# A two-layer trunk on one core: turned blocks fetched by SP's queue, work at fixed chunk distances, a buffer for the weights' turns

## The chip, the cores and the metric

The kernel runs on one core of one Trainium2 chip. The metric is the device time of one execution in microseconds. TensorE (PE) multiplies, VectorE (DVE) and ScalarE (ACT) do elementwise work, GpSimd (POOL) small arithmetic, and SyncE (SP) issues most transfers. Each engine takes its instructions in order.

## The reference

256 tokens of width 2048 pass two layers, each `h = h + Mixer(RMSNorm(h))`. Layer 1 is a gated DeltaNet. Layer 2, which the change touches, is banded softmax attention with 16 heads of 128; at 256 tokens the band holds every earlier chunk, so a frame sees its own 64-frame chunk and all before:

```
proj = h @ w_in                                  # q, k, v, gate z, 2048 wide each
q = rms_norm(q, q_norm_w); k = rms_norm(k, k_norm_w)
s = einsum('bchd,bmhd->bhcm', q_n, k_n) * scale + bias
p = softmax(where(valid, s, -inf))
o = einsum('bhcm,bmhd->bchd', p, v_n)
out = (o * silu(z)) @ w_out
```

All is float32.

## The kernel before

**Weights.** All weights (some 170 MB) are read once, in chunks of 512 KB. `fetch` (line 183) brings chunk after chunk on SP's queue into one of four buffers `wt`, ACT rounds it to a high part (`whi`, line 207, "the cast") and DVE subtracts for the low part (`wlo`, line 208). High and low parts have three buffers each. `chunk` (line 288) multiplies a chunk with the activations, which are split in the same way: three products. A wide chunk in layer 2 is twelve matmuls of 128x512. When chunk i is written, fetches up to i + 3 are written too, and `state["use"]` counts the chunks begun.

**The order.** Small work is written as generators in two lanes, `bgq` and `bg2`. A chunk gives two steps (`tick`); a step advances one lane, in turn, and a generator that yields 0 passes its step on. `behind` ties the work of a step behind the last matmul and the next chunk's cast and subtraction. The places on each engine follow from that when the program is built.

**Layer 2.** Its wide blocks have eight chunks each: keys and queries of a group of four heads in turn (K0, Q0, K1, Q1 to K3, Q3), then the values V0 to V3. That makes 96 chunks, numbered here from 0: K0 is 0 to 7, Q0 8 to 15, K1 16 to 23 and so on. The tokens lie on the partitions there; scores need the head's width on them. So a block is *turned*: DVE transposes it in pieces of 32x32 (line 1082), one DMA writes it to a scratch tensor in HBM (the *trip*, line 1053), and four DMAs *fetch* it back, 32 partitions each (line 1055). Both are issued by POOL, in `regroup`.

`qk_norm` (line 1058) is the chain of one K or Q block: square (ACT, line 1063), sum (DVE, 1066), reciprocal root (POOL, 1068 and 1070), normalising (DVE, 1075), turning, trip, fetch. Keys are fetched straight to `kn`; queries to a buffer `g` with the tag `cv`, from which ACT writes `qn` with a scale (line 1092, the *scaling pass*). `attend` (line 1095) is the chain of a group's four heads: scores (PE, 1112 and 1113; DVE 1122; ACT's exponentials, 1126), weights (DVE, 1132 and 1134), their turns by pairs of heads (DVE, 1141) with trip and fetch. It begins 11 chunks (`LEAD`) after its first step, and a step is one head. `values` (line 1166) multiplies weights by values.

The tag `cv` has two buffers, which squares, normalised blocks, turned blocks, `g` and the turned weights share. `kn`, `qn` and the values lie in the 48 KB slot `dl` (`hmem["m"]`), `kn` and `qn` with two places each.

Of the kernel before, what the change touches and what calls it, by code (L numbers as in the profile page):

```python
# [17 lines left out]
H = 16  # L18
# [6 lines left out]
LEAD = 11  # L25
# [14 lines left out]
def tile_hybrid_trunk(  # L40
# [11 lines left out]
    nc = tc.nc  # L52
# [35 lines left out]
    ps = ps_small()  # L88
# [74 lines left out]
    fetched, splits, state = {}, {}, {"next": 0, "use": 0, "mm": None}  # L163
# [52 lines left out]
    bgq, bg2, now = [], [], []  # L216
# [723 lines left out]
    for gi in range(4):  # L940
        ps = pair(xb, 2)
# [6 lines left out]
    hmem = {}  # L948
# [36 lines left out]
    bmem = {}  # L985

    def b_setup():
        scales["h"] = yield from row_scales(hmem["s"], "rh")
        ssh2 = scales["h"][2]
        uh = const.tile([P, 2], F32, name="uh")  # L990
        pool.tensor_scalar(out=uh, in0=ssh2, scalar1=1.0 / D, scalar2=EPS, op0=ALU.mult, op1=ALU.add)
        pool.tensor_scalar(out=uh, in0=uh, scalar1=EPS, scalar2=None, op0=ALU.mult)
        wqk = const.tile([P, 1], F32, name="wqk")
        pool.tensor_scalar(out=wqk, in0=sm[:, C_QW:C_QW + 1], scalar1=sm[:, C_KW:C_KW + 1],
                           scalar2=float(P) ** -0.5, op0=ALU.mult, op1=ALU.mult)
        bias = hmem["m"][:, 2 * D:4 * D].rearrange("p (h k) -> p h k", h=H)
# [49 lines left out]

    trips = [0]

    def regroup(dst, u):

        trips[0] += 1
        m = rows.tile([P, 4, 32 * u.shape[1]], F32, name="trip%d" % trips[0])
        nc.gpsimd.dma_start(out=m, in_=u.rearrange("p x c j -> p c (x j)"))
        for c in range(4):
            nc.gpsimd.dma_start(out=dst[32 * c:32 * c + 32].rearrange("i r x j -> i r (x j)"),  # L1055
                                in_=m[:, c, :].rearrange("(r i) y -> i r y", r=4))

    def qk_norm(ps, scale, dst):

        ssn = tiny.tile([P, 2, 4], F32, name="ssn", tag="so")  # L1060
        rn = tiny.tile([P, 2, 4], F32, name="rn", tag="ro")
        sq = wk("cv").rearrange("p h t -> p (h t)")
        act.activation(out=sq, in_=ps.rearrange("p t d -> p (t d)"), func=AF.Square)
        yield 1
        yield 1
        dve.reduce_sum(out=ssn, in_=sq.rearrange("p (t h d) -> p t h d", t=2, d=P), axis=AX.X)
# [3 lines left out]
        pool.tensor_tensor(out=rn, in0=ssn, in1=nhalf[:, :8].rearrange("p (t h) -> p t h", t=2), op=ALU.pow)  # L1070
        yield 1
        yield 1
        n = wk("cv").rearrange("p h t -> p (h t)").rearrange("p (t d) -> p t d", t=2)
        for t in range(2):
            dve.tensor_tensor(out=n[:, t, :].rearrange("p (h d) -> p h d", d=P),  # L1075
                              in0=ps[:, t, :].rearrange("p (h d) -> p h d", d=P),
                              in1=rn[:, t, :].unsqueeze(2).broadcast_to([P, 4, P]), op=ALU.mult)
        yield 1
        yield 1
        u = wk("cv").rearrange("p h t -> p (h t)").rearrange("p (c x j) -> p x c j", c=4, j=32)  # L1080
        for t in range(2):
            dve.transpose(out=u[:, 4 * t:4 * t + 4], in_=n[:, t, :].rearrange("p (x c i) -> p x c i", c=4, i=32))
            yield 1
        if scale is None:
            regroup(dst, u)
            yield 1
            return
        g = wk("cv").rearrange("p h t -> p (h t)").rearrange("p (r x j) -> p r x j", r=4, j=32)
        regroup(g, u)
        yield 1  # L1090
        yield 1
        act.activation(out=dst.rearrange("p x (r j) -> p r x j", r=4), in_=g, func=AF.Copy, scale=scale)
        yield 1

    def attend(gi, qn, kn):
        if gi == 0:
            gated_tiles()
            gmem["done"] = 0
            bmem["groups"] = 0
            bmem["w"] = slot("kT", 16)  # L1100
        st = {}
        first = state["use"] + LEAD
        while state["use"] < first:
            yield 0
# [30 lines left out]

        def turned(i):
            if i % 2 == 0:
                u = wk("cv").rearrange("p h t -> p (h t)")[:, :768]
                st["u"] = u.rearrange("p (c x j) -> p x c j", c=4, j=32)
            x = 3 * (i % 2)  # L1140
            dve.transpose(out=st["u"][:, x:x + 3], in_=st[i][0].rearrange("p (x c i) -> p x c i", c=4, i=32))
            if i % 2:
                regroup(weights_of((4 * gi + i) // 2), st["u"])

        stages = (scores, weights, turned)
        for n in range(4 + len(stages) - 1):
            for k in reversed(range(len(stages))):
                if 0 <= n - k < 4:
                    stages[k](n - k)
            yield 1  # L1150
        bmem["groups"] = gi + 1

    def weights_of(pr):

        w = bmem["w"][:, 768 * pr:768 * pr + 768] if pr < 5 else hmem["m"][:, 2 * D + 768 * (pr - 5):2 * D + 768 * (pr - 4)]
        return w.rearrange("p (r x j) -> p r x j", r=4, j=32)

    def vb_small(gi, ps):
        c = (8192, 10240, 9216, 11264)[gi]
        v = hmem["m"][:, c:c + 1024].rearrange("p (t d) -> p t d", t=2)  # L1160
        bmem["v"] = v
        for t in range(2):
            act.activation(out=v[:, t, :], in_=ps[:, t, :], func=AF.Copy, scale=scales["h"][0][:, t:t + 1])
        yield 1
# [33 lines left out]

    for gi in range(4):
# [30 lines left out]
    ps = [ps_small().rearrange("p (a t) -> p a t", a=2) for _ in range(2)]  # L1230
# [68 lines left out]
```

## Time and profile before

| | |
|---|---|
| median of 3 runs | 993.3 us (990.38 to 993.48) |
| the profiled execution | 992.0 us, its span 990.3 us |
| granted TensorE clock | 1.00 |
| DMA | 194.34 MB, mean 196 GB/s |
| ACT busy, POOL busy | 525.4 us, 114.8 us |
| chain that ended last | PE 85%, DMA 6%, DVE 3% |

Layer 2's wide blocks run from about 608 to 895 us. A row of the timeline has the start, the time taken, engine, line, operation, what it writes and reads, and in brackets the idle time of its engine before it and what ended that. Matmuls overlap, and their ends are modelled. A row of the stretches has the stretch, its length, the busy time and count of PE, PEld (weight loads), DVE, ACT and POOL, the granted clock, the busy share of the DMA engines and GB/s. DMAs issued by POOL appear as `trip<-cv` (the trip) and `cv<-trip`, `dl<-trip`, `kT<-trip` (fetches of queries, keys or weights, and weights).

### The profile page before, as it was taken

How to read it: one execution, taken by the hardware profiler on the slowest of the kernel's cores; microseconds unless marked ns; L12 is line 12 of the kernel's file. 1: busy time of each engine (PE TensorE's matmuls, PEld its weight loads, DVE VectorE, ACT ScalarE, POOL GpSimd, SP SyncE). 2: the span in 40 equal slices, each digit the busy share in tenths (PEclk: the TensorE clock that was granted, in tenths of full speed). 3: DMA queues.
4: the chain of work that ended last, by engine and by line, in shares of the span. 5: the costliest groups of instructions: out<-in, count | busy, mean ns of one | idle time of the engine just before them, and what ended most of it. 6: DMA issues, size and time to landing. Idle time of an engine off the chain costs nothing.

```text
span 990.3 us, 15268 instructions
## 1 busy us (share of the span) xinstructions
PE 979.2 (99%) x5803; PEld 849.7 (86%) x5803; DVE 699.5 (71%) x1146; ACT 525.4 (53%) x741; POOL 114.8 (12%) x177
## 2 busy tenths in 40 slices
PE   9999999999999999999999999999999999999998
PEld 7988888888888899899888888887788878888887
DVE  7789787997999768665767555555767766555544
ACT  8456887645547646444554444444454545444442
POOL 1002100122000001110000000122424240100000
PEclk9999999999999999999999999999999999999999
DMA  9668675545665553447765767686888786755672
GB/s 292 192 171 240 208 208 159 164 139 181 175 192 170 147 149 107 128 149 224 225 190 177 231 209 212 188 258 180 273 248 275 240 280 184 219 182 170 211 218 85
DMA packets 143817, 194.34 MB, mean 196 GB/s; under 512 B 9328, under 2 KB 100352, under 8 KB 143744
## 3 DMA queue, kind: packets, MB, share of 16 engines
q1 hardware_dynamic: 136832, 172.12, 57.4%
q0 software_dynamic: 6624, 20.99, 6.9%
q8 instruction: 45, 0.74, 0.3%
q10 hardware_dynamic: 288, 0.26, 0.1%
q14 instruction: 28, 0.23, 0.1%
HBM read 183.90 MB, written 9.45 MB: 195 GB/s over the span
## 4 chain that ended last, share of the span: by engine, by line
PE 85%; DMA 6%; DVE 3%; issue 2%; ACT 2%; POOL 2%; SPq 0%; ACTq 0%; DVEq 0%; POOLq 0%
PE psp L256 76%; DMA trip<-cv 3%; PE pss L602 2%; DVE wlo L208 1%; ACT whi L207 1%; DMA wt<-in_a_w_in_dram 1%; DMA wt<-in_b_w_in_dram 1%; PE pss L256 1%; PE pss L839 1%; PE pss L1175 1%; POOL rn L1070 1%; DMA cv<-trip 1%; DMA g<-in_xT_dram 1%; POOL ssn L1068 0%; PE pss L1113 0%
## 5 line engine op out<-in xcount | busy, mean ns | idle before, releaser
L208 DVE TENSOR_TENSOR wlo<-wt,whi 128x1024 fp32r<-128x1024 f32 (+2 forms) x324 | 390.0, 1208 | 222.7 <-ACT whi L207 221.3
L207 ACT CAST whi<-wt 128x1024 fp32r<-128x1024 f32 (+2 forms) x324 | 335.8, 1039 | 354.3 <-PE psp L256 309.0
L256 PE MATMUL psp<-whi,xb 128*128 128x512 f32 x1024 | 323.9, 394 | 0.4 <-ACT whi L207 0.4
L256 PE MATMUL psp<-xb,whi 128*128 128x512 f32 (+1 forms) x1088 | 257.5, 380 | 0.6 <-ACT whi L207 0.4
L256 PEld LDWEIGHTS psp<-whi,xb 128*128 128x128 f32 x1024 | 192.0, 188 | 39.9 <-ACT whi L207 0.8
L256 PEld LDWEIGHTS psp<-xb,whi 128*128 128x128 f32 x1088 | 195.3, 189 | 34.8 <-DVE ev L327 0.6
L256 PE MATMUL psp<-wlo,xb 128*128 128x512 f32 x512 | 200.8, 392 | 4.2 <-DVE wlo L208 4.2
L256 PE MATMUL psp<-xb,wlo 128*128 128x256 f32 x1024 | 147.3, 284 | 0.8 <-DVE wlo L208 0.5
L256 PEld LDWEIGHTS psp<-xb,wlo 128*128 128x128 f32 x1024 | 136.6, 191 | 7.2 <-DVE wlo L208 2.0
L256 PE MATMUL psp<-g,whi 128*128 128x512 f32 (+1 forms) x608 | 131.6, 346 | 0.2 <-DVE ev L327 0.2
L256 PEld LDWEIGHTS psp<-wlo,xb 128*128 128x128 f32 x512 | 96.2, 188 | 26.2 <-DVE wlo L208 6.8
L256 PEld LDWEIGHTS psp<-g,whi 128*128 128x128 f32 x608 | 104.4, 190 | 13.0 <-DVE ev L327 0.6
L256 PE MATMUL psp<-g,wlo 128*128 128x256 f32 x480 | 82.2, 283 | 0.0
L256 PEld LDWEIGHTS psp<-g,wlo 128*128 128x128 f32 x480 | 69.8, 191 | 1.8
L519 DVE SCALAR_TENSOR_TENSOR cv<-raw,sm,cv 128x255 f32<-128x255 f32 (+2 forms) x144 | 63.9, 480 | 5.2 <-ACT cv L517 4.9
L517 ACT ACTIVATE cv<-raw,sm 128x256 f32<-128x256 f32 x48 | 22.2, 501 | 10.4 <-DVE raw L342 10.4
L327 DVE TENSOR_TENSOR ev<-psp,ev 128x512 f32<-128x512 f32 x37 | 25.3, 683 | 0.1
L326 ACT COPY ev<-psp 128x512 f32<-128x512 f32 x37 | 21.4, 579 | 2.5 <-DVE raw L342 2.5
L874 POOL TENSOR_TENSOR ro<-so,nhalf 128x8 f32<-128x8 f32 x4 | 8.4, 2107 | 122.4 <-DVE so L872 122.4
L1075 DVE TENSOR_TENSOR cv<-psp,rn 128x512 f32<-128x512 f32 x16 | 10.3, 685 | 12.4 <-POOL rn L1070 12.4
L1055 POOL DMA_DIRECT2D dl<-trip x28 | 15.4, 558 | 27.8 <-DMA trip<-cv 22.4
L1126 ACT ACTIVATE raw<-raw,mx 128x128 f32<-128x128 f32 (+1 forms) x32 | 14.3, 446 | 7.6 <-DVE mx L1124 7.6
(245 smaller groups left out, 750.5 us busy)
## 6 DMA issues: line engine op xcount, KB each, us to landing
wt<-in_b_w_in_dram SPq DMA_DIRECT2D x128, 512.0 KB, 4.4
wt<-in_a_w_in_dram SPq DMA_DIRECT2D x125, 512.0 KB, 4.0
wt<-in_a_w_out_dram SPq DMA_DIRECT2D x32, 512.0 KB, 3.7
wt<-in_b_w_out_dram SPq DMA_DIRECT2D x32, 512.0 KB, 3.4
trip<-cv POOLq DMA_DIRECT2D x8, 512.0 KB, 5.3
trip<-cv POOLq DMA_DIRECT2D x8, 384.0 KB, 4.3
tt<-line POOLq DMA_DIRECT2D x4, 512.0 KB, 9.5
dl<-in_xT_dram POOLq DMA_DIRECT2D x4, 512.0 KB, 6.5
```

The costliest lines, as they stand in the source:

```text
L207: cast = act.copy(out=hi[:, js, cs], in_=wt[:, js, cs])
L208: rest = dve.tensor_tensor(out=lo[:, js, cs], in0=wt[:, js, cs], in1=hi[:, js, cs].bitcast(F32), op=ALU.subtract)
L256: state["mm"] = pe.matmul(*args, **kw).ins
L326: act.copy(out=ev, in_=ps[:, :, 1, :])
L327: dve.tensor_tensor(out=ev, in0=ps[:, :, 0, :], in1=ev, op=ALU.add)
L517: act.activation(out=cv[:, i, :], in_=raw[:, i, :], func=AF.Copy, scale=conv_w(i0 + i, 3))
L519: dve.scalar_tensor_tensor(out=cv[:, i, s:], in0=raw[:, i, :T - s], scalar=conv_w(i0 + i, 3 - s), in1=cv[:, i, s:], op0=ALU.mult, op1=ALU.add)
L602: pe.matmul(dst, lhsT=kq[:, a, i, c:c + P], rhs=rhs, start=(n == 0), stop=(n == 2))
L839: pe.matmul(ps[:, i * P:(i + 1) * P], lhsT=tt[:, 2 * (h0 + i) + t, :], rhs=vb[:, i, t, :], start=True, stop=True)
L1055: nc.gpsimd.dma_start(out=dst[32 * c:32 * c + 32].rearrange("i r x j -> i r (x j)"), in_=m[:, c, :].rearrange("(r i) y -> i r y", r=4))
L1075: dve.tensor_tensor(out=n[:, t, :].rearrange("p (h d) -> p h d", d=P), in0=ps[:, t, :].rearrange("p (h d) -> p h d", d=P), in1=rn[:, t, :] ...
L1126: act.activation(out=s[:, a:b], in_=s[:, a:b], func=AF.Exp, bias=mx[:, t:t + 1], accum_out=sums[:, t:t + 1])
```

## The change

`regroup` becomes two functions. `trip` writes the block to HBM, still from POOL; `back` fetches it, now from SP's queue. Between them stands `until`, which holds a generator until `state["use"]` has reached a number: for a block that ended at `end`, the fetch waits for `end + 7`, the scaling pass for `end + 10`, and head n of the group for `end + 11 + 2n` (a step of two chunks a head, with an empty step between a pair's trip and its fetch). Counters `scored` and `turned` keep the pass and the scores of neighbouring groups apart, since `qn` now has one place. Its second place holds the turned weights, which leave `cv`.

```diff
+    def trip(u):
         trips[0] += 1
         m = rows.tile([P, 4, 32 * u.shape[1]], F32, name="trip%d" % trips[0])
         nc.gpsimd.dma_start(out=m, in_=u.rearrange("p x c j -> p c (x j)"))
+        return m
+    def back(dst, m):
         for c in range(4):
-            nc.gpsimd.dma_start(out=dst[32 * c:32 * c + 32].rearrange("i r x j -> i r (x j)"),
-                                in_=m[:, c, :].rearrange("(r i) y -> i r y", r=4))
+            nc.sync.dma_start(out=dst[32 * c:32 * c + 32].rearrange("i r x j -> i r (x j)"),
+                              in_=m[:, c, :].rearrange("(r i) y -> i r y", r=4))
+    def until(use):
+        while state["use"] < use:
+            yield 0
...
+        m = trip(u)
+        yield from until(end + LEAD - 4)
         if scale is None:
-            regroup(dst, u)
+            back(dst, m)
             yield 1
             return
         g = wk("cv")...
-        regroup(g, u)
-        yield 1
-        yield 1
+        back(g, m)
+        yield from until(end + LEAD - 1)
+        while bmem["scored"] < bmem["turned"]:
+            yield 0
+        bmem["turned"] += 1
         act.activation(out=dst..., in_=g, func=AF.Copy, scale=scale)
...
-        first = state["use"] + LEAD
-        while state["use"] < first:
-            yield 0
...
-                u = wk("cv").rearrange("p h t -> p (h t)")[:, :768]
+                st["u"] = hmem["m"][:, 11264:12032].rearrange("p (c x j) -> p x c j", c=4, j=32)
...
-                regroup(weights_of((4 * gi + i) // 2), st["u"])
+                st["m", i] = trip(st["u"])
+        def fetched_(i):
+            if i % 2:
+                back(weights_of((4 * gi + i) // 2), st["m", i])
-        stages = (scores, weights, turned)
+        stages = (scores, weights, turned, None, fetched_)
+        while bmem["turned"] <= gi:
+            yield 0
         for n in range(4 + len(stages) - 1):
+            bmem["scored"] = gi + (n >= 4)
+            yield from until(end + LEAD + 2 * n)
...
-        c = (8192, 10240, 9216, 11264)[gi]
+        c = 8192 + 1024 * gi
...
-        qn = hmem["m"][:, 10240 + c:11264 + c].rearrange("p (x t) -> p x t", x=8)
-        bgq.append(qk_norm(psk, None, kn))
+        qn = hmem["m"][:, 10240:11264].rearrange("p (x t) -> p x t", x=8)
+        bgq.append(qk_norm(psk, None, kn, state["use"]))
         psq = block("tokens", xb)
-        bgq.append(qk_norm(psq, bmem["wqk"][:, 0:1], qn))
-        bg2.append(attend(gi, qn, kn))
+        bgq.append(qk_norm(psq, bmem["wqk"][:, 0:1], qn, state["use"]))
+        bg2.append(attend(gi, qn, kn, state["use"]))
```

Lines behind it move: the square is line 1072, the sum 1075, the roots 1077 and 1079, normalising 1084, turns 1091 and 1150, the pass 1105, scores 1122, 1123 and 1132, exponentials 1136, fetches 1059.

What this does to the order is seen at three places. On ACT, from the square of Q0 on, with casts in between; before:

```order
L1063 ACTIVATE cv<-psp 128x1024
L207 CAST whi<-wt 128x1024 x7
L1092 ACTIVATE dl<-cv,wqk 128x4x8x32
L207 CAST whi<-wt 128x1024
L1063 ACTIVATE cv<-psp 128x1024
L207 CAST whi<-wt 128x1024 x4
```

and now:

```order
L1072 ACTIVATE cv<-psp 128x1024
L207 CAST whi<-wt 128x1024 x8
L1105 ACTIVATE dl<-cv,wqk 128x4x8x32
L1072 ACTIVATE cv<-psp 128x1024
L207 CAST whi<-wt 128x1024 x3
```

Q0's scaling pass stood before cast 26 and stands before cast 27, in front of K1's square. The passes of Q1 to Q3 keep their places, before casts 43, 59 and 75.

On POOL, the group of K1 and Q1 (each trip's number is the buffer's); before, with the fetches (four each) between:

```order
L1053 DMA trip_6818<-cv 128x1024
L1055 DMA dl<-trip_6818 32x4x256 x4
L1053 DMA trip_6837<-cv 128x768
L1055 DMA kT<-trip_6837 32x4x192 x4
L1053 DMA trip_6880<-cv 128x768
L1068 TENSOR_SCALAR ssn<-ssn,uh 128x4 x2
L1070 TENSOR_TENSOR rn<-ssn,nhalf 128x8
L1055 DMA kT<-trip_6880 32x4x192 x4
L1053 DMA trip_6992<-cv 128x1024
L1055 DMA cv<-trip_6992 32x4x256 x4
```

and now POOL has only trips and roots, while the fetches of the same blocks stand on SP between the weight fetches (the row of nineteen ends with fetch 18):

```order
L1053 DMA trip_6847<-cv 128x1024
L1053 DMA trip_6873<-dl 128x768
L1077 TENSOR_SCALAR ssn<-ssn,uh 128x4 x2
L1079 TENSOR_TENSOR rn<-ssn,nhalf 128x8
L1053 DMA trip_6980<-dl 128x768
L1053 DMA trip_7009<-cv 128x1024
```

```order
L181 DMA wt<-in_b_w_in_dram 128x2x512 x19
L1059 DMA dl<-trip_6421 32x4x256 x4
L181 DMA wt<-in_b_w_in_dram 128x2x512 x8
L1059 DMA cv<-trip_6588 32x4x256 x4
L181 DMA wt<-in_b_w_in_dram 128x2x512 x10
L1059 DMA dl<-trip_6847 32x4x256 x4
L181 DMA wt<-in_b_w_in_dram 128x2x512 x2
L1059 DMA kT<-trip_6873 32x4x192 x4
L181 DMA wt<-in_b_w_in_dram 128x2x512 x4
L1059 DMA kT<-trip_6980 32x4x192 x4
L181 DMA wt<-in_b_w_in_dram 128x2x512
L1059 DMA cv<-trip_7009 32x4x256 x4
```

Sixteen blocks of four fetches moved. K1's stands before weight fetch 37, its group's pairs before 39 and 43, Q1's before 44; the next groups repeat that 16 fetches on.

On DVE, from the sum of K1 to its second turn, before:

```order
L1066 TENSOR_REDUCE ssn<-cv 128x8
L208 TENSOR_TENSOR wlo<-wt,whi 128x1024
L1075 TENSOR_TENSOR cv<-psp,rn 128x512 x2
L208 TENSOR_TENSOR wlo<-wt,whi 128x1024
L1082 STREAM_TRANSPOSE cv<-cv 128x4x4x32
L208 TENSOR_TENSOR wlo<-wt,whi 128x1024
L1082 STREAM_TRANSPOSE cv<-cv 128x4x4x32
```

and now, with the first heads' scores and weights in between:

```order
L1075 TENSOR_REDUCE ssn<-cv 128x8
L1132 ISA raw,mx<-pss,dl 128x128
L1132 ISA mx 128x1
L1132 ISA raw,mx<-pss,dl 128x256
L1132 ISA mx 128x1
L1134 TENSOR_SCALAR mx<-mx 128x2
L208 TENSOR_TENSOR wlo<-wt,whi 128x1024
L1142 RECIPROCAL sums<-sums 128x2
L1144 TENSOR_SCALAR raw<-raw,sums 128x128
L1144 TENSOR_SCALAR raw<-raw,sums 128x256
L1084 TENSOR_TENSOR cv<-psp,rn 128x512 x2
L208 TENSOR_TENSOR wlo<-wt,whi 128x1024
```

The sum of K1 stands two `wlo` later than before (`wlo` 27 was next, 29 is now), and a head is worked on in every second chunk instead of every chunk. Q1's second turn, which shared a place with its first behind `wlo` 36, stands behind `wlo` 38. On PE the scores of a group's first head stand up to a chunk earlier: those of group 1 at chunk 42 behind nine of its twelve matmuls, where they stood at chunk 43 behind six.

More of the change, by code (lines that the diff above doesn't have):

```diff
@@ L997, in b_setup @@
         bmem.update(uh=uh, wqk=wqk, bias=bias,
-                    z=slot("tt", 16).rearrange("p (h t) -> p h t", h=H))
+                    z=slot("tt", 16).rearrange("p (h t) -> p h t", h=H), scored=0, turned=0)
         yield 1
@@ L1047, in tile_hybrid_trunk @@
     trips = [0]
-    def regroup(dst, u):
+    def trip(u):
         trips[0] += 1
@@ L1053, in regroup, with qk_norm @@
         nc.gpsimd.dma_start(out=m, in_=u.rearrange("p x c j -> p c (x j)"))
+        return m
+    def back(dst, m):
         for c in range(4):
-            nc.gpsimd.dma_start(out=dst[32 * c:32 * c + 32].rearrange("i r x j -> i r (x j)"),
-                                in_=m[:, c, :].rearrange("(r i) y -> i r y", r=4))
-    def qk_norm(ps, scale, dst):
+            nc.sync.dma_start(out=dst[32 * c:32 * c + 32].rearrange("i r x j -> i r (x j)"),
[3 more added lines that the diff above has]
+            yield 0
+    def qk_norm(ps, scale, dst, end):
         ssn = tiny.tile([P, 2, 4], F32, name="ssn", tag="so")
@@ L1088, in qk_norm, with attend @@
         g = wk("cv").rearrange("p h t -> p (h t)").rearrange("p (r x j) -> p r x j", r=4, j=32)
-        regroup(g, u)
-        yield 1
-        yield 1
+        back(g, m)
[3 more added lines that the diff above has]
+        bmem["turned"] += 1
         act.activation(out=dst.rearrange("p x (r j) -> p r x j", r=4), in_=g, func=AF.Copy, scale=scale)
         yield 1
-    def attend(gi, qn, kn):
+    def attend(gi, qn, kn, end):
         if gi == 0:
@@ L1137, in turned @@
             if i % 2 == 0:
-                u = wk("cv").rearrange("p h t -> p (h t)")[:, :768]
-                st["u"] = u.rearrange("p (c x j) -> p x c j", c=4, j=32)
+                st["u"] = hmem["m"][:, 11264:12032].rearrange("p (c x j) -> p x c j", c=4, j=32)
             x = 3 * (i % 2)
@@ L1142, in turned @@
             if i % 2:
-                regroup(weights_of((4 * gi + i) // 2), st["u"])
-        stages = (scores, weights, turned)
+                st["m", i] = trip(st["u"])
[5 more added lines that the diff above has]
+            yield 0
         for n in range(4 + len(stages) - 1):
+            bmem["scored"] = gi + (n >= 4)
+            yield from until(end + LEAD + 2 * n)
             for k in reversed(range(len(stages))):
-                if 0 <= n - k < 4:
+                if stages[k] and 0 <= n - k < 4:
                     stages[k](n - k)
```

## The prediction

> **What bounds the kernel now.** First the busy times and the stretches of the program.
>
> ```profile
> PE 979.2 (99%) x5803; PEld 849.7 (86%) x5803; DVE 699.5 (71%) x1146; ACT 525.4 (53%) x741; POOL 114.8 (12%) x177
> 160.00:530.00 370.00, 370.00 (x2609) 329.51 (x2608) 297.01 (x524) 202.11 (x276) 29.83 (x26) 1.00 0.56 168
> 640.00:815.00 175.00, 170.38 (x755) 139.16 (x755) 116.73 (x203) 83.23 (x118) 55.37 (x88) 1.00 0.81 249
> 815.00:900.00 85.00, 85.00 (x401) 71.48 (x400) 48.82 (x88) 41.81 (x64) 7.16 (x14) 1.00 0.65 199
> ```
>
> TensorE is busy for 99% of the span at full granted clock (1.00), so only its holes can be won. The stretch 640 to 815 us, where the queries and keys of layer 2 are turned and the scores made, has 175.00 - 170.38 = 4.62 us of them; before and behind it there are none. The timeline of PE shows every hole there:
>
> ```profile
> 650.04 0.61 PE L256 MATMUL psp<-whi,xb 128*128 128x512 f32 x2
> 650.49 0.39 PE L256 MATMUL psp<-wlo,xb 128*128 128x512 f32 x1
> 650.72 0.61 PE L256 MATMUL psp<-whi,xb 128*128 128x512 f32 x2
> ...
> 678.70 0.50 PE L256 MATMUL psp<-whi,xb 128*128 128x512 f32 x1 [0.40 <-ACT whi L207]
> 679.96 0.50 PE L256 MATMUL psp<-wlo,xb 128*128 128x512 f32 x1 [0.76 <-DVE wlo L208]
> 686.81 0.49 PE L256 MATMUL psp<-wlo,xb 128*128 128x512 f32 x1 [0.45 <-DVE wlo L208]
> 712.48 0.50 PE L256 MATMUL psp<-wlo,xb 128*128 128x512 f32 x1 [1.54 <-DVE wlo L208]
> 779.01 0.50 PE L256 MATMUL psp<-wlo,xb 128*128 128x512 f32 x1 [0.56 <-DVE wlo L208]
> 807.44 0.50 PE L256 MATMUL psp<-wlo,xb 128*128 128x512 f32 x1 [0.88 <-DVE wlo L208]
> ```
>
> Undisturbed, three matmuls take 0.68 us (650.04 to 650.72), so one starts each 0.227 us while it is booked for 0.39. A hole therefore costs 0.39 - 0.227 = 0.16 us beyond its idle time, and the first matmul behind it 0.11 more (0.50 for 0.39). The six holes: 4.59 + 6 x 0.27 = 6.2 us. That is the **ceiling of any gain**. A chunk of weights, twelve matmuls, is 2.72 us.
>
> What makes the holes is read on ACT and POOL:
>
> ```profile
> 667.46 1.05 ACT L207 CAST whi<-wt 128x1024 fp32r<-128x1024 f32 x1 [1.67 <-PE psp L256]
> 670.18 1.05 ACT L207 CAST whi<-wt 128x1024 fp32r<-128x1024 f32 x1 [1.67 <-PE psp L256]
> 676.56 1.15 ACT L1092 ACTIVATE dl<-cv,wqk 128x1024 f32<-128x1024 f32 x1 [5.33 <-DMA cv<-trip]
> 677.62 1.03 ACT L207 CAST whi<-wt 128x1024 fp32r<-128x1024 f32 x1
> 704.44 1.03 ACT L1063 ACTIVATE cv<-psp 128x1024 f32<-128x1024 f32 x1 [3.51 <-DMA trip<-cv]
> ...
> 770.11 1.06 ACT L207 CAST whi<-wt 128x1024 fp32r<-128x1024 f32 x1 [0.63 <-PE psp L256]
> 775.61 1.15 ACT L1092 ACTIVATE dl<-cv,wqk 128x1024 f32<-128x1024 f32 x1 [3.53 <-DMA cv<-trip]
> 776.67 1.98 ACT L207 CAST whi<-wt 128x1024 fp32r<-128x1024 f32 x2
> 671.27 1.23 DVE L208 TENSOR_TENSOR wlo<-wt,whi 128x1024 fp32r<-128x1024 f32 x1 [1.50 <-ACT whi L207]
> 704.70 2.19 POOL L1055 DMA_DIRECT2D kT<-trip  x4 [6.72 <-DMA trip<-cv]
> 708.32 1.66 POOL L1070 TENSOR_TENSOR rn<-ssn,nhalf 128x8 f32<-128x8 f32 x1
> 710.01 1.29 DVE L1075 TENSOR_TENSOR cv<-psp,rn 128x512 f32<-128x512 f32 x2 [2.16 <-POOL rn L1070]
> ```
>
> Cast c starts when PE has done chunk c - 3 (three buffers); the `lo` part ends 671.27 + 1.23 - 670.18 = 2.32 us later. PE needs both two chunks, 5.44 us, after the cast's start. So a cast may be **3.1 us late** for nothing, and each further microsecond is a hole. The rows bear it out: cast 26 began at 677.62, 2.72 us after 670.18 would have been 672.90: 4.7 late, 1.6 lost by this rule, and the two first holes are 1.16 + 2 x 0.27 = 1.7. Cast 59 (776.67 for 772.83) is 3.8 late, 0.7 by the rule, 0.56 + 0.27 in the trace. So two kinds of hole: ACT stands at the query's scaling pass (L1092) until the fetched block lands (678.70, 679.96, its echo at 686.81, 779.01); and POOL stands at a fetch (704.70), so that the reciprocal roots behind it (708.32), DVE's scaling (710.01) and the next `lo` come late (712.48, in the same way 807.44).
>
> **The change, part by part.** Chunks are numbered 0 to 95 in layer 2's wide blocks (K0 is 0 to 7, Q0 8 to 15, K1 16 to 23 and so on); t is the undelayed start of cast 38.
>
> *POOL.* The 64 fetches leave it. Behind a trip's issue nothing waits for a landing any more, so the roots start when DVE's sum is there. Both holes of the second kind go: 1.54 + 0.88 + 2 x 0.27 = 3.0 us. What is late next is DVE itself, whose pieces are these:
>
> ```profile
> 679.83 1.21 DVE L1066 TENSOR_REDUCE ssn<-cv 128x8 f32<-128x1024 f32 x1
> 686.67 0.70 DVE L1082 STREAM_TRANSPOSE cv<-cv 128x512 f32<-128x512 f32 x1
> 689.03 0.25 DVE L1122 CUSTOM_DVE_ANT_0 raw<-pss,dl 128x128 f32<-128x128 f32 x1
> 689.75 1.23 DVE L208 TENSOR_TENSOR wlo<-wt,whi 128x1024 fp32r<-128x1024 f32 x1
> 691.52 0.54 DVE L1134 TENSOR_SCALAR raw<-raw,sums 128x128 f32<-128x128 f32 x2
> 692.10 0.58 DVE L1141 STREAM_TRANSPOSE cv<-raw 128x384 f32<-128x384 f32 x1
> ```
>
> A head's scores take 0.72 (689.03 to 689.75). The chunk with the sum (1.21), scores and `lo` (1.23) has 3.2 us; the next (weights 0.6, L1075 1.29, `lo`) 3.1; then 2.7 and 3.1: 12.1 for four chunks of 2.72, a backlog of 1.2, with a few tenths for ACT's exponentials about 1.7 us, under 3.1. In the old order each of four chunks in a row held a head's scores and weights; now every second does.
>
> *The turns' own buffer.* The square of the queries waited 3.51 us at 704.44 for a trip to be read out of `cv`. That wait goes; it lies on the same path as the hole at 712.48 and is not counted twice. The new buffer is single: the second pair's first turn waits for the first pair's trip, by my tally within 0.3 us of its landing, and the 3.1 us cover it.
>
> *Q0's pass* moves behind one more cast (before cast 27). Trip and landing as in the trace until 667.7; SP then issues four blocks.
>
> ```profile
> 668.21 2.19 POOL L1055 DMA_DIRECT2D cv<-trip  x4 [5.61 <-DMA trip<-cv]
> L181 SPq DMA_DIRECT2D wt<-in_b_w_in_dram x40: 367/368/368, 702.2 to 818.1; - x40
> DMA to landing us min/median/max: 3.7/5.2/8.7
> L1053 POOL DMA_DIRECT2D trip<-cv x16: 563/570/633, 640.3 to 844.8; - x16
> DMA to landing us min/median/max: 2.6/5.3/7.1
> DMA to landing us min/median/max: 2.3/4.3/7.5
> L1092 ACT ACTIVATE dl<-cv,wqk x4: 1150/1152/1157, 676.6 to 822.1; 128x1024 f32<-128x1024 f32 x4
> ```
>
> The three landing rows are, in order, of the weight fetches on SP, the trips out and the fetches back. POOL's last of four issues began at 668.21 + 3 x 0.55 = 669.9; ACT was released at 676.56, 6.7 us later. On SP an issue takes 0.37 us: the last one begins at about 668.8 and lands, by the same 6.7, at 675.5. Pass (1.15) and square (1.03) follow, so cast 27 starts at 677.6 for 672.90 + 2.72 = 675.62: **2.0 late, no hole**. The holes at 678.70, 679.96 and 686.81 go: 1.61 + 0.8 = 2.4 us.
>
> *Q1 to Q3's pass* stays before casts 43, 59, 75, but the turns ahead of it come later: Q1's second turn now stands behind `lo` 38, where both stood behind `lo` 36. `lo` 38 ends at t + 2.3, with the rest of the backlog up to 3.4; turn 0.70; trip 5.3; three issues on SP 1.1; landing, between 2.3 and 7.5 on POOL's queue. I take **5.2**, the median of the queue that it moves to: t + 14.6 to 15.7. With the pass cast 43 starts at t + 15.8 to 16.9 for t + 13.6, 2.2 to 3.3 late: no hole or 0.2. At 2.3 none at all, at 7.5 it is 4.5 to 5.6 late, some 1.4 to 2.5 + 0.3 lost in each of three groups. Of the hole at 779.01 (0.8) I count 0.2 given back at each Q.
>
> [...]
>
> *SP.* Fetch c leaves when DVE has let go of buffer c - 4, 10.9 - 2.3 = 8.6 us ahead of cast c. Landing 5.2, so 3.4 us are spare, and 3.1 more behind the cast: 6.5. Now SP stands at each block until its trip has landed, and the weights queue behind it. Worst are K1 to K3, before fetches 37, 53, 69. With u for the start of cast 31: turns done at u + 5.2, trip landed at u + 10.5, four issues to u + 12.0; fetch 37 would leave at u + 7.7. **4.3 late, of 6.5.** At the Q blocks fetch 44 leaves at about t + 11.0 for 7.8, 3.2 late; at the pairs 1 to 2. I take 0.2 us lost per K for the crowding. At the slow ends, a trip of 7.1 and a fetch of 8.7, it is 4.3 + 1.8 + 3.5 - 6.5 = 3.1 us per K; at the quick ones nothing.
>
> *PE's own order.* The scores stand up to a chunk earlier (Q1's first head at chunk 42, nine of twelve matmuls in, for 43 and six). PE gets there at t + 10.9 + 5.4 + 2.0 = t + 18.3, the pass is done by t + 16.9: 1.4 us to spare, nothing gained.
>
> **Sum.** 6.2 - 3 x 0.2 - 3 x 0.2 = 5.0 us less. The profiled execution took 992.0 us (span 990.3 and 1.7 around it), so 987.0 by its own time; the runs' median is 993.3 (990.38 to 993.48), and the forecast stands against it: **988.3**.
>
> **Rivals.** *The landing stays slow* (same): the blocks take 7.5 us on SP as well. Then Q1 to Q3 lose 1.7 to 2.8 each, 6.7 in all, and the 6.2 are gone: 993.3 + 0.5 = 993.8; with Q0's 6.7 it is 0.8 less each, 991.4. For: POOL's slow landings fell beside three weight fetches, and the DMA share is 0.81 in this stretch. Against: on SP's own queue no later fetch stands ahead of them.
>
> *SP becomes the bound* (slower). Fetches at 8.7 lose 4.3 + 3.5 - 6.5 + 0.3 = 1.6 at each K and 0.5 at each Q, and with the landing of the first rival 2.2 more: 3 x 4.3 = 12.9, less 6.2: 1000.0. It starts where trip and fetch together pass 5.3 + 5.2 + 2.2 = 12.7 us, and outweighs the 6.2 where a group loses 2.1. [...] Against: 8.7 was one fetch of 40.
>
> That the distances are not what the text says can be left out: the order has the blocks and passes where I counted them.
>
> **How the numbers follow.** Forecast 0.58, slow landing 0.27, SP as the bound 0.15. A measurement of this kernel can tell about 0.3%, 3.0 us, from no change. The forecast reaches from 987.1 (all of 6.2) to 990.3, the slow landing from there to 994. The runs' own spread of 3 us widens the lower end to 985.5; the upper end is 995.5, since nearly all that is left out is the slower case. Faster 0.58, same 0.28, slower 0.14.
>
> **What would show it.** Right: no hole on PE between 640 and 815 us beyond 0.3 us; ACT's waits at the pass near 2 us; POOL without waits for a trip's landing; SP standing 3 to 4 us at each block, and casts that still wait for PE rather than for weights. Wrong: casts that wait for `wt`, or PE holes behind chunks 37, 43, 53, 59, 69, 75. What would make it wrong is a landing of the blocks, or of the fetches behind them, above 6.5 us.

## The result and the profile after

The changed kernel takes **985.96 us** (median of 15 runs, 984.48 to 989.20), the kernel before in the same series 991.25 us (15 runs, 989.12 to 993.89). The ratio is **0.9949, 95% interval 0.9938 to 0.9960**: 5.3 us or 0.5% faster. The profiled execution took 986.99 us with a span of 985.3, 5.0 less than the profiled execution before.

The page's busy times and the stretches of the program, in the columns of before:

```profile
PE 978.8 (99%) x5803; PEld 850.7 (86%) x5803; DVE 700.6 (71%) x1146; ACT 525.5 (53%) x741; POOL 84.1 (9%) x113
640.00:815.00 175.00, 174.20 (x778) 143.76 (x777) 120.13 (x205) 85.89 (x121) 29.53 (x35) 1.00 0.84 253
815.00:900.00 85.00, 85.00 (x405) 71.47 (x405) 49.84 (x93) 41.97 (x67) 1.08 (x2) 1.00 0.65 196
```

TensorE's idle time between 640 and 815 us fell from 4.62 to 0.80 us, and 23 more matmuls fit there (778 for 755). POOL's 64 DMA issues are gone (113 instructions for 177). What is left of the holes, in PE's timeline:

```profile
728.28 0.50 PE L256 MATMUL psp<-wlo,xb 128*128 128x512 f32 x1 [0.20 <-DVE wlo L208]
...
773.50 0.49 PE L1122 MATMUL pss<-dl 128*128 128x128 f32 x2 [0.25 <-ACT dl L1105]
...
775.69 0.50 PE L256 MATMUL psp<-wlo,xb 128*128 128x512 f32 x1 [0.34 <-DVE wlo L208]
```

All three stand behind the scaling passes of Q1 and Q2; the starts of the matmuls show 0.2 us lost behind Q3's as well. ACT's timeline has Q0's pass and Q1's:

```profile
673.73 1.15 ACT L1105 ACTIVATE dl<-cv,wqk 128x1024 f32<-128x1024 f32 x1
674.79 1.00 ACT L1072 ACTIVATE cv<-psp 128x1024 f32<-128x1024 f32 x1
675.69 1.03 ACT L207 CAST whi<-wt 128x1024 fp32r<-128x1024 f32 x1
...
708.18 1.05 ACT L207 CAST whi<-wt 128x1024 fp32r<-128x1024 f32 x1 [1.62 <-PE psp L256]
...
724.88 1.16 ACT L1105 ACTIVATE dl<-cv,wqk 128x1024 f32<-128x1024 f32 x1 [3.85 <-DMA cv<-trip]
725.94 2.99 ACT L207 CAST whi<-wt 128x1024 fp32r<-128x1024 f32 x3
```

Q0's pass waits for nothing. Q1's waits 3.85 us for its block, and cast 43 starts at 725.94, where five chunks after cast 38 would be 708.18 + 5 x 2.72 = 721.78: 4.2 us late, with 0.20 us of idle time on PE to show for it.

The waits, of the queue on SP over the whole span (the first two rows) and of the engines from 640 to 850 us; a row has who waits, for whom, the sum in us, how often, and the longest:

```profile
SPq L1059 <- DMA trip<-dl: 19.4, 7, 4.6
SPq L1059 <- DMA trip<-cv: 15.5, 6, 4.2
ACT dl L1105 <- DMA cv<-trip: 12.3, 3, 4.5
ACT whi L207 <- DMA wt<-in_b_w_in_dram: 7.7, 4, 2.8
DVE cv L1084 <- POOL rn L1079: 3.6, 3, 1.8
```

POOL's waits for landings have become SP's, 35 us in 13 waits, where they hold up weight fetches and not roots. Four casts wait for weights, 7.7 us in all, without a hole on PE.

### The profile page after: what moved, and what is told of

The parts are those of the page before. It is cut to its first block, busy times and chain, and to the rows that moved or that the text cites. A ratio compares the mean times of both kernels' runs of the same rounds, so it can differ in the third digit from the quotient of the medians.

```text
span 985.3 us, 15237 instructions
## 1 busy us (share of the span) xinstructions
PE 978.8 (99%) x5803; PEld 850.7 (86%) x5803; DVE 700.6 (71%) x1146; ACT 525.5 (53%) x741; POOL 84.1 (9%) x113
## 4 chain that ended last, share of the span: by engine, by line
PE 87%; DMA 5%; DVE 3%; ACT 2%; issue 1%; SPq 1%; POOL 0%; ACTq 0%; DVEq 0%
PE psp L256 78%; DMA wt<-in_b_w_in_dram 2%; PE pss L602 2%; DVE wlo L208 2%; DMA trip<-cv 1%; ACT whi L207 1%; DMA wt<-in_a_w_in_dram 1%; PE pss L256 1%; PE pss L839 1%; PE pss L1192 1%; DMA g<-in_xT_dram 1%; PE pss L1123 0%; PE pss L738 0%; PE pss L825 0%; PE pss L862 0%
## 5 line engine op out<-in xcount | busy, mean ns | idle before, releaser
L606 DVE TENSOR_TENSOR dl<-pss,dl 128x512 f32<-128x512 f32 (+1 forms) x32 | 16.4, 546 | 1.7 <-PE pss L602 1.7
L1077 POOL TENSOR_SCALAR ssn<-ssn,uh 128x4 f32<-128x4 f32 x16 | 8.2, 526 | 99.8 <-DVE ssn L1075 91.1
```

The lines of the kernel that those rows point to most:

```text
L606: dve.tensor_tensor(out=dl[:, h, :, c], in0=src.rearrange("p (k c) -> p k c", k=2), in1=dec[:, h, c].unsqueeze(1).broadcast_to([P, 2, n]), ...
```

## The experiments

Each has its own runs of the kernel before beside it; the ratio is to those, with its 95% interval.

| | median us | ratio |
|---|---|---|
| e1 queue alone | 991.25 | 1.0012 (0.9999 to 1.0025) |
| e2 fetches back on POOL's queue | 1004.49 | 1.0144 (1.0125 to 1.0162) |
| e3 turns back in `cv` | 993.71 | 1.0038 (1.0020 to 1.0055) |
| e4 no distances | 996.19 | 1.0062 (1.0038 to 1.0086) |
| e5 POOL, SP held | 1004.25 | 1.0143 (1.0122 to 1.0163) |
| e6 POOL, heads later | 990.38 | 1.0001 (0.9987 to 1.0014) |
| e7 two passes | 990.83 | 1.0007 (0.9989 to 1.0026) |
| e8 one chunk later | 984.78 | 0.9946 (0.9932 to 0.9961) |
| e9 POOL, SP held longer | 992.34 | 1.0026 (1.0013 to 1.0038) |
| e10 one chunk later, three groups | 985.16 | 0.9952 (0.9940 to 0.9964) |
| e11 the changed kernel again | 985.83 | 0.9960 (0.9948 to 0.9972) |
| e12 three passes | 993.05 | 1.0032 (1.0019 to 1.0044) |

### e1: the queue alone

The kernel before with one edit:

```diff
-            nc.gpsimd.dma_start(out=dst[32 * c:32 * c + 32].rearrange("i r x j -> i r (x j)"),
-                                in_=m[:, c, :].rearrange("(r i) y -> i r y", r=4))
+            nc.sync.dma_start(out=dst[32 * c:32 * c + 32].rearrange("i r x j -> i r (x j)"),
+                              in_=m[:, c, :].rearrange("(r i) y -> i r y", r=4))
```

> The kernel before with its fetches on SP's queue and nothing else. Theory (the distances make the gain): POOL is free, so the two holes behind the roots go (3.0 us), but the built order now has the scaling pass before casts 25, 41, 57, 73, one to two casts earlier than before, so ACT waits for the landing there: Q1 to Q3 lose 1.5 to 3 us each. Ratio to the kernel before 0.998 to 1.003. Rival (the queue makes the gain): the pass is served early by the faster landing, and the ratio is that of the change, 0.995.

The waits of e1, ACT's from 640 to 850 us and PE's over the whole span (0.7 us of PE's two rows lie outside these bounds):

```profile
ACT dl L1092 <- DMA cv<-trip: 23.5, 4, 7.8
PE psp L256 <- ACT whi L207: 5.3, 4, 3.1
PE psp L256 <- DVE wlo L208: 2.6, 5, 0.8
```

No gain: 1.0012, as the theory had it. POOL's holes are gone, but in the built order the pass of Q1 to Q3 stands before casts 41, 57 and 73 instead of 43, 59 and 75, ACT waits there up to 7.8 us for the block (before: 5.3), and three groups of holes behind these passes give back what was won. The trace is of the slowest of the twelve runs, 996.35 us, which also has, by its mean clock (0.84 from 760 to 780 us, 0.99 from 780 to 800), some 6.8 us at half clock; the five runs at a clock of 1.000 take 988.14 to 991.51.

### e2: the changed kernel with the fetches on POOL

```diff
-            nc.sync.dma_start(out=dst[32 * c:32 * c + 32].rearrange("i r x j -> i r (x j)"),
+            nc.gpsimd.dma_start(out=dst[32 * c:32 * c + 32].rearrange("i r x j -> i r (x j)"),
```

> The changed kernel with its fetches back on POOL's queue; distances and buffer kept. Theory (distances): Q1's roots come when POOL is already through with K1's fetch, and the pass, here before casts 44, 60, 76, has one more cast, so the holes stay near 0 to 0.6 us per Q: within 1.5 us of the changed kernel, ratio to the kernel before 0.994 to 0.997. Rival (queue): POOL stands at each landing again and the roots and the landings come late: 3 to 5 us back, ratio 0.998 to 1.000.

Neither: 1.0144, slower than anything foreseen. PE's timeline at Q1's scores and the waits:

```profile
726.92 0.61 PE L256 MATMUL psp<-whi,xb 128*128 128x512 f32 x2
731.27 0.49 PE L1122 MATMUL pss<-dl 128*128 128x128 f32 x2 [3.73 <-ACT dl L1105]
...
733.20 1.05 PE L256 MATMUL psp<-whi,xb 128*128 128x512 f32 x2
734.05 0.63 PE L256 MATMUL psp<-wlo,xb 128*128 128x512 f32 x1
```

```profile
ACT dl L1105 <- DMA cv<-trip: 22.1, 4, 7.1
PE pss L1122 <- ACT dl L1105: 11.0, 3, 4.3
```

Two things are new. PE stands at the scores itself, which are in its own order: 3.73 us here, 11.0 in three groups, and the main matmuls behind the scores start only at 731.84. And behind that hole two matmuls take 0.85 us (733.20 to 734.05) instead of 0.45: the granted clock has fallen to half (0.51 from 732.59 to 736.01). That is taken up in the last section. What is open is why the block lands so late on POOL's queue; e5 and e9 are for that.

### e3: the turned weights back in `cv`

```diff
-                st["u"] = hmem["m"][:, 11264:12032].rearrange("p (c x j) -> p x c j", c=4, j=32)
+                st["u"] = wk("cv").rearrange("p h t -> p (h t)")[:, :768].rearrange("p (c x j) -> p x c j", c=4, j=32)
```

> The changed kernel with the turned weights in cv again; queue and distances kept. Theory: the square of Q1 to Q3 waits for the pair's trip, about 3 us at ACT before casts 35, 51, 67, of which 3.1 are covered: within 1 us of the changed kernel, ratio to before 0.994 to 0.996. Rival (the buffer is what freed the path of the hole at 712): a hole of 1 to 2 us per group comes back, ratio 0.997 to 1.000.

1.0038, above both expectations: without the buffer the gain is gone and 3.8 us more. The waits of e3 (PE's row behind `wlo` is over the whole span; 2.9 us of it lie between 640 and 850):

```profile
ACT dl L1105 <- DMA cv<-trip: 16.9, 3, 6.3
DVE cv L1091 <- DMA trip<-cv: 10.5, 3, 4.6
PE psp L256 <- DVE wlo L208: 3.7, 8, 1.0
PE pss L1122 <- ACT dl L1105: 3.1, 2, 1.8
```

DVE now stands at the queries' turns (line 1091) until an older trip has been read out of `cv`, three times; in the changed kernel it never does. Q1's trip is issued at 714.54, in the changed kernel at 711.40. It lands sooner, 4.2 us after its issue for 5.8, so Q1's pass starts only 1.0 us later (725.89 for 724.88); behind it the delays add up, and Q2's pass starts 3.9 us later (776.19 for 772.29).

### e4: no distances

```diff
-        yield from until(end + LEAD - 4)
...
-        yield from until(end + LEAD - 1)
+        yield 1
+        yield 1
...
+        first = state["use"] + LEAD
+        while state["use"] < first:
+            yield 0
...
-        stages = (scores, weights, turned, None, fetched_)
+        stages = (scores, weights, turned, fetched_)
...
-            yield from until(end + LEAD + 2 * n)
```

> The changed kernel without the distances: fetch, pass and heads follow one another as before; queue and buffer kept. Theory (distances): the pass stands before casts 25, 41, 57, 73 and waits for the landing, so Q1 to Q3 lose 1.5 to 3 us each: ratio to before 0.998 to 1.003. Rival (queue and buffer): as the changed kernel, 0.995.

1.0062, a little worse than expected. The pass stands before casts 41, 57 and 73, as in e1 (PE's rows are over the whole span, with 1.7 us that lie outside 640 to 850; the trace is of the slowest run, 1000.47 us, and has three stretches of half clock: its mean is 0.91 from 720 to 740 us, 0.92 from 760 to 780 and 0.91 from 820 to 840):

```profile
ACT dl L1105 <- DMA cv<-trip: 24.3, 4, 7.3
PE psp L256 <- ACT whi L207: 6.5, 4, 2.4
PE psp L256 <- DVE wlo L208: 3.7, 7, 0.8
```

So at these distances none of the three parts can be left out, and the queue alone wins nothing; only together they are faster. Whether other distances would make up for a missing part was not tried for the buffer; for the queue, e6 and e9 come back to the time before, and not below it.

### e5 and e9: why the block lands late on POOL's queue

Both are e2 with small reads of the trip by SP, so that SP stands there until the trip has landed and weight fetches behind it wait. e5 has one, e9 has six at the queries' blocks:

```diff
+        hold = tiny.tile([1, 48], F32, name="hold", tag="hold")
+        for c in range(n):
+            nc.sync.dma_start(out=hold[:, 8 * c:8 * c + 8], in_=m[0:1, 0, 8 * c:8 * c + 8])
```

> As e2 (the fetches back stand on POOL's queue), but SP also reads 8 numbers of every trip at the place where the fetches stood, so that it waits for the trip's landing there and the weight fetches behind it are held back as in the changed kernel. Theory 'holding back' (the blocks are quick on SP because the weights stand still behind them): blocks of Q1 to Q3 land in 5 to 6.5 us, where e2 had 7.6 to 8.3; PE's wait at the scores falls from 11.0 us to under 4; 0.996 to 1.001 of the time before, the rest of the changed kernel's gain being lost to POOL's in-order waits. Rival 'POOL's queue is slow by itself': blocks land in 7.5 us or more as in e2, PE's wait at the scores stays near 11 us, 1.012 to 1.017.

> As e5, but at the queries' blocks SP reads six small pieces of the trip instead of one, so that the next weight fetch leaves some 2 us after the trip's landing, when POOL has issued all four blocks: the order that SP's own queue gives in the changed kernel. (In the built order the scaling pass comes one cast later than in e5.) e5 showed 5 us for the first block, issued before the weights, and 7.3 to 8.4 for those issued beside them. Theory 'what is issued first lands first': all four blocks of Q1 to Q3 land in 3 to 6.3 us; PE's wait at the scores falls from 10.3 us to under 4; 0.998 to 1.006 of the time before. Rival 'POOL's queue is slow for such blocks': the last blocks still land in 7.3 us or more and the time stays at 1.010 or above.

Q2's block in each, by line 1059 and by SP's timeline. The first of two rows gives the count, how long one issue takes in ns (least, median, most) and when the first and the last issue start, the second the landing; SP's have start, duration and count.

In the changed kernel:

```profile
L1059 SPq DMA_DIRECT2D cv<-trip x4: 303/424/430, 764.7 to 766.0; - x4
DMA to landing us min/median/max: 5.3/5.9/6.2
```

In e2:

```profile
L1059 POOL DMA_DIRECT2D cv<-trip x4: 550/550/552, 773.8 to 775.4; - x4
DMA to landing us min/median/max: 7.4/7.8/8.0
```

In e5, with SP's rows:

```profile
L1059 POOL DMA_DIRECT2D cv<-trip x4: 550/551/552, 772.5 to 774.1; - x4
DMA to landing us min/median/max: 5.1/7.6/8.0
```

```profile
771.93 0.58 SPq L1062 DMA_DIRECT2D hold<-trip  x2
772.61 4.97 SPq L181 DMA_DIRECT2D wt<-in_b_w_in_dram  x4
```

In e9, with SP's rows:

```profile
L1059 POOL DMA_DIRECT2D cv<-trip x4: 552/552/552, 767.5 to 769.1; - x4
DMA to landing us min/median/max: 3.1/3.2/5.3
```

```profile
766.92 2.03 SPq L1063 DMA_DIRECT2D hold<-trip  x7
769.05 2.74 SPq L181 DMA_DIRECT2D wt<-in_b_w_in_dram  x4
```

(Each SP row counts one more read, of the second pair's trip.) e5 seemed to speak for "POOL's queue is slow": 1.0143, and up to 8.0 us. But its reads let SP go at 772.61, while POOL, at 0.55 us an issue, still had three of four fetches to issue; only the first, ahead of the weights, took 5.1 us. In e9 the weights leave at 769.05, just as POOL begins the last of the four, and the four land in 3.1 us at the least, 3.2 by the median and 5.3 at the most. Q1 (4.1 to 5.4) and Q3 (3.9 to 5.4) read the same. In e2 a weight fetch leaves at 772.72, ahead of the block's first issue at 773.8, and the block takes 7.4 to 8.0. So POOL's queue alone doesn't make the landing slow: **in these runs a block issued ahead of the weights lands sooner than one issued beside them**. How much of the quick landing is due to the weight fetches ahead of the block, these runs don't tell apart. The time falls from 1.0143 to 1.0026, though in e9 the pass also comes a cast later, so the fall isn't due to the landing alone. e9 has two holes, of 1.05 us at 754.22 and of 3.24 us at 802.09. Behind the second is this wait:

```profile
803.59 0.58 DVE L1153 STREAM_TRANSPOSE dl<-raw 128x384 f32<-128x384 f32 x1 [5.95 <-DMA trip<-dl]
```

DVE stands at the turn of the second pair's weights until the first pair's trip has landed, and this trip was issued behind K3's four fetches on POOL. So the order on SP does two things at once: Q2's block goes ahead of the weights (from 764.73, they from 766.56), and on POOL no trip stands behind a block.

### e6: the heads later on POOL's queue

```diff
-            yield from until(end + LEAD + 2 * n)
+            yield from until(end + LEAD + 2 + 2 * n)
```

In e6 and e8 the scores of the last head come behind the copy of V1 into the place of its keys, so this head is scored against values; kinds, sizes and number of the instructions are the same.

> As e2, but each head's scores two chunk distances later; in the built order PE's first scores of a group stand about one chunk (12 matmuls, 2.72 us) later. Theory 'PE waits directly at the scores and pays again by the clock': of e2's waits of 3.7 to 4.3 us there 2.7 go in each of three groups, and with the long holes the stretches at granted clock 0.50 go too: 19 us over the changed kernel fall to 5 to 9, 0.999 to 1.005 of the time before, no row at a clock under 0.9. Rival 'the late pass itself is the bound, over cast 44': the holes move to the main matmuls behind a late cast and the time stays at 1.010 or more.

1.0001, 14 us less than e2 and as the theory had it. From 640 to 850 us PE's waits at the scores are gone, 2.7 us behind `wlo` and 1.4 behind a cast remain, and so does one stretch of half clock (a mean of 0.91 from 780 to 800 us), where none was expected and e2 has three. ACT still stands at the pass for up to 7.2 us, so most of e2's loss was PE's direct wait and what the clock adds to it, and not the late pass by itself.

### e7 and e12: the pass done twice and three times

```diff
-        act.activation(out=dst.rearrange("p x (r j) -> p r x j", r=4), in_=g, func=AF.Copy, scale=scale)
+        for _ in range(2):
+            act.activation(out=dst.rearrange("p x (r j) -> p r x j", r=4), in_=g, func=AF.Copy, scale=scale)
```

e12 has 3 for 2. In the built order the second pass stands behind the cast that follows the first, so the scores wait for both.

> The changed kernel with the scaling pass done twice: 1.05 to 1.15 us more on ACT at each Q, the output unchanged up to the factor applied (the second pass writes the same values). Theory 'cushion' (a cast may be some 4 to 5 us late at Q1 to Q3, the 3.1 us and the four heads' matmuls, and all of it is used up): Q0 takes it for nothing, Q1 to Q3 lose about 1.0 us each, 0.9975 to 0.9990 of the time before. Rival 'ACT still has room there': 0.9940 to 0.9955, as the changed kernel.

1.0007, above what the theory gave (0.9975 to 0.9990), with an interval that reaches into it. The 12 runs fall into groups by the granted clock: five at 1.000 take 986.74 to 988.47, five at 0.998 take 990.01 to 992.62, two at 0.996 take 993.29 and 993.78. The five lie, by their median of 987.88, 2.0 us above e11's 985.83 (the kernel before took 989.38 beside e7 and 989.42 beside e11), less than the some 3 us expected. The others are slower and have a lower clock; one such stretch costs 1.7 us by estimate (last section), so by this they have longer holes too; no trace of theirs shows it.

> The changed kernel with the scaling pass done three times (the same values each time); in the built order the second and third stand behind the cast that follows the first, so the scores of Q1 to Q3 wait 1.05 us longer than in e7. Theory 'clock by windows': in all runs so far the granted clock fell to 0.50 for the next 3.41 us exactly when PE had been idle for more than about 1.7 us within one window of 3.41 us (13 windows with 0.7 to 1.72 us idle and no fall at full clock, 9 with 1.76 to 3.36 and a fall); so here the two or three groups whose holes reach 1.8 us in one window fall, and only those; 1.003 to 1.010 of the time before, more than the 1.002 that 3.2 us on top of e7's quicker runs would give. Rival 'a single idle time of about 3.4 us is needed': no fall, since no hole is that long, and 1.001 to 1.003.

The counts of windows in this expectation are a tally, in part miscounted; the last section has the windows that views show. The time, 1.0032 (1.0019 to 1.0044), lies just inside the theory's range, and its interval reaches well into the rival's, so the time doesn't decide. All six runs have a clock of 0.998 or 0.996, and the trace has a fall without any hole of 3.4 us (the longest is 3.0), which speaks against the rival; the last section shows it.

### e8, e10 and e11: pass and heads one chunk later

```diff
-        yield from until(end + LEAD - 1)
+        yield from until(end + LEAD - 1 + late)
...
-            yield from until(end + LEAD + 2 * n)
+            yield from until(end + LEAD + (gi < 3) + 2 * n)
```

This is e10, with `late` 1 for the first three groups; e8 has it in all four.

> The changed kernel with pass and heads one chunk later (pass before casts 28, 44, 60, 76, each head one chunk distance on). Theory 'cushion': the casts in front of the pass no longer wait for its block, the remaining holes (some 1.5 us) go, 0.9925 to 0.9945 of the time before. Rival 'the holes only move' (blocks land behind each other, weights held back longer): 0.995 to 0.999.

> e8 for the first three groups alone (pass and heads one chunk later), the last group as in the changed kernel, so that its heads stay ahead of the values that take the keys' place. Theory 'cushion': the holes of Q1 and Q2 go, those of Q3 (0.2 us) stay: 0.9930 to 0.9950 of the time before, 1.0 to 1.5 us under the changed kernel. Rival 'they only move': the time of the changed kernel or above.

> The changed kernel again, beside e10 on the same chip: 0.9938 to 0.9960 of the time before, as in its first runs.

No hole is left in either: PE is busy for all of the 175 us from 640 to 815, and of the 85 behind them. Both times still lie just above the ranges expected, 0.9946 for at most 0.9945 in e8 and 0.9952 for at most 0.9950 in e10. e10's runs, 984.54 to 985.67, lie 0.7 us by the median below e11's, 985.48 to 986.42, on the same chip, where 1.0 to 1.5 were expected. The intervals of the ratios overlap, so this much is likely and not settled. e10 is faster than the kernel before and at least level with the changed one. e11 itself, 0.9960, stands at the end of the range expected, and its interval overlaps the first one (0.9938 to 0.9960).

## Why the prediction was right, point by point

Forecast 5.0 us less and 988.3 us, measured 5.3 less (ratio 0.9949) and 985.96; the profiled executions differ by 5.0. Of the 2.3 us between forecast and result 2.05 are the reference: the forecast stood against a median of 993.3 from three runs, and 15 runs of the kernel before gave 991.25. So 985.96 lies only 0.5 us above the lower end of the range (985.5), while the gain itself was met to 0.3 us. The holes and what removes them were read rightly. That the sum came so near is in part luck, since two of its terms were off in opposite ways: the scaling passes lose more than was counted, SP's waits nothing.

The traces give the sum between two fixed places, the starts of cast 0 and of cast 95, which is the last of layer 2's wide blocks: 284.4 us before, 279.5 in the changed kernel, 278.0 in e10 and 279.3 in e11.

- **Ceiling, 6.2 us.** Borne out: e10 has no hole left, and between the two casts it takes 6.3 us less than the kernel before.
- **POOL, 3.0 us.** As predicted. DVE waits 3.6 us in three times for the roots, and no hole follows.
- **The turns' own buffer**, counted at nothing beyond POOL's hole. In the change as a whole that holds, and DVE waits for no trip at it. Alone it was under-rated: e3 is 0.0089 of the time, 8.8 us, above the changed kernel, and its queries' turns wait 10.5 us for older trips.
- **Q0's pass, 2.0 us late and no hole.** No hole, and only 0.2 late (675.69 for 670.06 + 2 x 2.72 = 675.50): its block landed 2.8 to 3.7 us after its issue, where 6.7 was carried over from POOL's queue. The term of 2.4 us stands.
- **Q1 to Q3's pass, 2.2 to 3.3 late, 0.2 us lost each.** This term was mis-sized. The casts came 4.2, 4.8 and 4.5 late, mainly since the last blocks took 6.0 to 6.3 us for the 5.2 taken. By the cushion of 3.1 that would be 1.1 to 1.7 us each; measured are 0.5, 1.1 and 0.2, the idle time with 0.27 for each hole (0.2 at Q3 by the starts alone). What the rule left out is PE's own work in between: a head's scores stand just there, 0.57 us (773.50 to the next main matmul at 774.07), which leaves 0.5 and 1.1 for Q1 and Q2, as measured, and at Q3 products with the values stand there as well. In e11, the same kernel again, Q1's cast comes 3.0 late and no hole follows; Q2's comes 4.3 late, and its one hole costs 0.36 + 0.27, the 0.6 that is left of 4.3 less 3.1 and 0.57. The three lose 1.8 us by their holes instead of 0.6, and 1.5 by the distance of the changed kernel from e10 between the two casts (e11: 1.3, and 0.7 by the medians). 6.3 less 1.5 is the 4.8 by which the two kernels differ there.
- **SP at K1 to K3, 4.3 late of 6.5 spare, 0.2 lost each.** No hole, so nothing of the 0.6 was lost. Fetch 37 left 2.3 us late, 53 and 69 left 3.6 and 3.2 late; the fetches behind the blocks took up to 8.6 us to land, and the casts' waits for weights (7.7 us) used up the spare time without passing it. The rival that makes SP the bound did not come, though e9, with SP held longer, shows waits for weights of 15.2 us. The prediction's own signs of being wrong were set too tight: it named casts that wait for `wt`, holes behind chunks 43 and 59, and landings above 6.5 us among others, and these came without costing the gain.
- **PE's own order, 1.4 us to spare.** PE got to Q1's scores at 726.34, t + 18.2, as predicted (18.3), but the pass ended at 726.04: 0.3 to spare, and at Q2 PE waited 0.25. This was the tightest place, where 1.4 was counted, and e2 shows its price: there the pass starts at 730.07 and PE stands for 3.73 us.
- **The landing.** 5.2 us was taken, with 7.5 as the rival. On SP the blocks of Q1 to Q3 take 5.1 to 6.3 us, against 7.4 to 8.3 in e2. POOL's queue alone doesn't make them slow: in e9 they land on it in 3.1 to 5.4 us, issued ahead of the weights or just as these leave. In the changed kernel Q2's block leaves from 764.73 and the next weights from 766.56; in e2 a weight fetch leaves at 772.72 and the block from 773.8. The prediction's reason, that no later fetch stands ahead on SP's own queue, agrees with this, and its "slow landing" stayed a rival.

What the prediction had not seen is how far the parts need each other: it summed them singly, while e2 to e4 show that each missing part, with all else left in place, costs all of the gain and 4 to 14 us more, and e1 that the queue by itself brings nothing.

## What to carry to other kernels

Where short transfers on a critical chain run beside a stream that has slack, try to issue both from one queue. Here SP's waits at the trips (35 us in 13) held the weight fetches back, Q2's block landed in 5.3 to 6.2 us instead of 7.4 to 8.0 (e2), and the casts' waits for weights (7.7 us) left no hole on PE. Give each instruction that waits for a landing a place by counted chunks, and see what stands behind it in its engine's order: by the prediction's estimate a cast here can be 3.1 us late for nothing, while in e2 PE lost 3.73 us at the scores and the fall of the clock on top. And test parts of a change together as well as singly, since here no part could be left out, at the distances chosen, without losing all.

## What the runs showed of the hardware

**Where the granted clock fell.** e2 has three stretches at half clock. By estimate from its mean clock (0.70 from 731 to 735 us, 0.87 to 739; 0.99 from 778 to 784, 0.50 to 788, 0.67 to 792; 0.68 from 837 to 841, 0.89 to 845) they begin at 732.6, 783.9 and 838.4 us and last 3.4, 6.8 and 3.4; from one start to the next it is about 15 and 16 times 3.41 us. Cut into windows of this length, the stretches of e2 around Q1 (idle time is the length less PE's busy time; the column behind POOL is the granted clock):

```profile
725.77:729.18 3.41, 1.76 (x8) 1.13 (x6) 0.00 (x0) 0.00 (x0) 0.00 (x0) 1.00 1.04 257
729.18:732.59 3.41, 1.32 (x7) 1.19 (x8) 0.41 (x1) 2.52 (x3) 0.00 (x0) 1.00 0.36 124
732.59:736.01 3.42, 3.42 (x10) 2.64 (x9) 3.42 (x7) 0.51 (x1) 1.28 (x3) 0.51 0.40 97
```

The hole of 3.73 us is split, 1.65 in the first window and 2.09 in the second, and the fall follows the second. In e9 no fall follows a hole of 3.24 us. At the borders put here, which no fall in that trace confirms, it is split as well, 1.69 and 1.55:

```profile
800.37:803.78 3.41, 1.72 (x8) 1.10 (x6) 0.19 (x1) 1.04 (x1) 0.00 (x0) 1.00 0.96 320
803.78:807.19 3.41, 1.86 (x8) 1.55 (x9) 3.41 (x5) 0.00 (x0) 2.26 (x4) 1.00 0.51 107
807.19:810.61 3.42, 3.42 (x17) 2.82 (x16) 3.42 (x6) 1.06 (x1) 0.57 (x1) 1.00 0.89 276
```

In e6 a fall follows 1.76 us:

```profile
776.88:780.30 3.42, 1.66 (x7) 0.84 (x6) 1.47 (x2) 3.42 (x4) 0.00 (x0) 1.00 0.72 189
780.30:783.71 3.41, 3.41 (x10) 2.73 (x10) 2.02 (x2) 0.40 (x1) 2.33 (x3) 0.51 0.58 166
```

e12, run after its expectation was put down, has both cases:

```profile
771.30:774.71 3.41, 2.22 (x10) 1.50 (x8) 0.23 (x1) 2.35 (x3) 0.00 (x0) 1.00 1.04 365
774.71:778.12 3.41, 2.65 (x11) 1.98 (x11) 1.46 (x2) 3.38 (x4) 0.00 (x0) 1.00 0.41 111
822.49:825.90 3.41, 0.50 (x1) 0.19 (x1) 0.83 (x1) 3.41 (x4) 0.00 (x0) 1.00 0.60 222
825.90:829.32 3.42, 2.97 (x7) 2.40 (x8) 1.90 (x3) 3.10 (x4) 0.00 (x0) 0.50 0.49 141
829.32:832.73 3.41, 3.41 (x19) 3.00 (x19) 2.24 (x6) 1.04 (x1) 0.00 (x0) 1.00 0.72 213
```

At Q2 the idle time of 1.95 us is cut into 1.19 and 0.76, and no fall follows; at Q3 2.91 us in one window are followed by half clock in the next. That agrees with the expectation, though only one group fell and not two or three (the run's mean clock is 0.998); the longest single hole there is 3.0 us. In the windows shown, idle time of 0.76 to 1.69 us was followed by no fall, and 1.76 (e6), 2.09 (e2) and 2.91 us (e12) by one; more than these few windows is not shown. e12's window at half clock with 0.45 us of idle time was followed by full clock; in e2, with 0.77 us from 784 to 788 at 0.50, the stretch lasted 6.8 us. At half clock two matmuls take 0.85 us for 0.45 (e2), so by estimate a stretch at half clock costs half its length, 1.7 or 3.4 us, on top of the hole.

So in these traces the longer hole was not always the dearer one: 3.24 us in e9 brought no fall, 2.91 in e12 did. The spread of e7's runs by clock, 986.74 to 993.78, agrees with this, though only one of them has a trace. e8 and e10, without holes, spread over 0.6 and 1.1 us. The kernel before spreads over 5 us, mostly at a clock of 1.000, so this isn't all of its spread; the rest stays open.
